# First expert's rows gathered by columns, unread products on TensorE during the top-k, and logits scaled and shifted in one operation per tile

## The chip, the cores and the metric

The kernel runs on one core of one Trainium2 chip. The metric is the device time of one execution in microseconds (us). "PE" is TensorE's matmul stream and "PEld" its weight loads, "DVE" is VectorE, "ACT" is ScalarE, "POOL" is GpSimd, and "SP" is SyncE, whose queue issues the weight transfers. An f32 product of the program appears in the trace as two loads and two matmul instructions (128 instructions for 64 products of one line, say); a transpose appears as one of each.

## The reference, cut to what matters

One encoder block: attention branches, then an expert-choice feed-forward over 16 experts, then a final norm. The change lies between the two halves.

```python
def expert_choice_ffn(h, w_router, w_gate, w_up, w_down):     # h: (1, 512, 1024)
    cap = EC_CAPACITY_FACTOR * S // N_EXPERTS                 # 64 rows for each of 16 experts
    aff = jax.nn.softmax((h @ w_router).astype(jnp.float32), axis=-1)
    gate, idx = lax.top_k(jnp.swapaxes(aff, 1, 2), cap)
    xe = h[bidx, idx]                                         # the rows each expert takes
    hid = (jax.nn.silu(jnp.einsum('becd,edf->becf', xe, w_gate))
           * jnp.einsum('becd,edf->becf', xe, w_up))          # w_gate, w_up: (16, 1024, 2048)
    ye = jnp.einsum('becf,efd->becd', hid, w_down) * gate[..., None]
    return jnp.zeros_like(h).at[bidx, idx].add(ye)
...
h2 = rmsnorm(x, g_norm_ffn[l]) * (1.0 + sc2) + sh2
x = x + gt2 * expert_choice_ffn(h2, ...)
```

## The kernel before

The first 900 us compute the attention half. From about 895 us on the kernel streams the expert weights: 12 tiles of 2 MB for each expert (per quarter of the 1024 inputs one of `w_gate` and one of `w_up`, then four of `w_down`), 192 tiles in all, through a ring of ten slots (`wslot`, `RING`). `loaded` (L1055) asks for the first ten tiles at once; SP's queue issues each later tile in program order, and it waits there until PE has read the tile that its slot held. So the eleventh tile cannot start before the first expert's first gate products (the first 16 instructions of L1199) are done, since they free the first slot.

Between the attention half and those products stands a chain of small steps:

1. `route(j)` gives for each of four tiles of 128 tokens the router's logits `lg[:, j]` and the sum of squares; `rsqrt_mean` makes the reciprocal norm `rs`. L1068 multiplies all logits by `rs`, L1069 adds the row `lbb`. POOL makes the normed tokens `xn` from `rs` at the same time (L1071).
2. Softmax (L1074 to L1079), a transpose on PE (L1084), and the top-k on DVE: eight rounds of `max` (L1089, eight largest) and seven of `match_replace` (L1091). The threshold goes back through PE (L1100) to `thb`; the positions `pos` follow from prefix sums on PE (L1111, L1113) and small DVE steps to L1123.
3. `select(0)` compares `pos` with an iota, four DVE operations (L1141): `gw[:, j]` is a 128 x 64 matrix of zeros and ones, tokens by places.
4. `gather(0, gw)` multiplies it with `xn`: `gw[:, j]` is the stationary operand (64 columns), 512 columns of `xn` move; 8 products, both halves of the array at once. The result `px` holds places by model columns.
5. `rows(px)` copies it to SBUF (L1155), transposes it in four products (L1158), then scales by `a2c` (L1160) and shifts by `sh2c` (L1162) on DVE: `xT[:, k]`, 128 model columns by 64 places, is the stationary operand of every gate and up product.

Two sets of small products that the first expert needs only later, L1207 (`tpb` from `gw` and the identity) and L1213 (`tpb` from `gw` and `aff`), stand between `rows` and the gate products on PE. Where instructions of different steps stand on an engine is decided by the scheduler from the order in which the program is written and from its own forecast of waits.

Of the kernel before, what the change touches and what calls it, by code (L numbers as in the profile page):

```python
# [9 lines left out]
F32 = mybir.dt.float32  # L10
# [4 lines left out]
OP = mybir.AluOpType  # L15
# [4 lines left out]
P = 128  # L20
S = 512
D = 1024
KD = D // P
NT = S // P
# [3 lines left out]
E_N = 16  # L28
CAP = 64
# [72 lines left out]
def tile_block(ctx, tc, x, c, positions, w_ada, b_ada, g_norm_mix, w_in, g_q_lat, g_kv_lat, w_uq, w_ukv,  # L102
               rel_bias, w_out, g_norm_ffn, w_router, w_gate, w_up, w_down, g_final, consts, masks, out):
    nc = tc.nc
    V, A, G, T, SP = nc.vector, nc.scalar, nc.gpsimd, nc.tensor, nc.sync
# [14 lines left out]
    x1 = per.tile([P, NT, D], F32, name="x1")  # L120
# [6 lines left out]
    a2c = per.tile([P, KD], F32, name="a2c")  # L127
# [26 lines left out]
    with ExitStack() as pa:  # L154
# [16 lines left out]
        def sc():  # L171
            return ps.tile([P, 512], F32, name="sc", bufs=3)
# [892 lines left out]

        xn = keep.tile([P, NT, D], F32, name="xn")
        rs = rsqrt_mean(ss2, NT, D, keep, "rs2")
        V.tensor_tensor(lg, lg, rs[:, :, None].to_broadcast([P, NT, E_N]), op=OP.mult)  # L1068
        V.tensor_tensor(lg, lg, lbb[:, None, :].to_broadcast([P, NT, E_N]), op=OP.add)  # L1069
        for j in range(NT):  # L1070
            G.tensor_scalar(xn[:, j], x1[:, j], rs[:, j:j + 1], None, op0=OP.mult)  # L1071
        aff = keep.tile([P, NT, E_N], F32, name="aff")
# [11 lines left out]
            T.transpose(pt[:64, 128 * a:128 * a + 128], afx[:, a], ident)  # L1084
        V.tensor_copy(at, pt[:64, :256])
        m64 = wk.tile([64, CAP], F32, name="m64")
        for r in range(CAP // 8):
            m8 = m64[:, 8 * r:8 * r + 8]
            V.max(m8, at)  # L1089
            if r < CAP // 8 - 1:  # L1090
                V.match_replace(at, m8, at, -1.0)  # L1091
        rev = wk.tile([E_N, CAP], F32, name="rev")
# [7 lines left out]
        T.matmul(pq[:, :E_N], onesr[:E_N], dth, start=True, stop=True)  # L1100
        thb = wk.tile([P, E_N], F32, name="thb")
        V.tensor_copy(thb, pq[:, :E_N])

        ge2 = wk.tile([P, NT, 2, E_N], BF16, name="ge2")
        tb_ = thb[:, None, :].to_broadcast([P, NT, E_N])
# [9 lines left out]
        V.tensor_copy(pre[:, NT, 0], pq[:, 128:144])  # L1115
        eqp = wk.tile([P, NT, E_N], F32, name="eqp")
        V.tensor_tensor(eqp, pre[:, :NT, 1], pre[:, NT, 0][:, None, :].to_broadcast([P, NT, E_N]), op=OP.add)
        t1 = wk.tile([P, NT, E_N], F32, name="t1")
        V.scalar_tensor_tensor(t1, eqp, float(CAP) + 0.5, eqp, op0=OP.is_lt, op1=OP.mult)
        V.tensor_mul(t1, t1, ge2[:, :, 1])  # L1120
# [7 lines left out]
    with ExitStack() as pb_:  # L1128
# [15 lines left out]
        def gather(e, gw):  # L1144
            px = ps.tile([P, 512], F32, name="px", bufs=1)
            for j in range(NT):
                for dh in range(2):
                    T.matmul(px[64 * dh:64 * dh + 64], gw[:, j], xn[:, j, 512 * dh:512 * dh + 512],  # L1148
                             start=j == 0, stop=j == NT - 1)
            return px  # L1150

        def rows(px):

            xe = wbs.tile([P, 4, P], F32, name="xe", tag="xy", bufs=1)
            V.tensor_copy(xe, px.rearrange("q (p r) -> q r p", r=4))  # L1155
            pt = ps.tile([P, 512], F32, name="tpb", bufs=2)
            for n in range(4):
                T.transpose(pt[:, 128 * n:128 * n + 128], xe[:, n], ident)  # L1158
            xT = wbs.tile([P, KD, CAP], F32, name="xT", bufs=1)
            V.tensor_tensor(xT.rearrange("p (h n) s -> p n h s", h=2), pt.rearrange("p (n h s) -> p n h s", n=4, h=2),  # L1160
                            a2c.rearrange("p (h n) -> p n h", h=2)[:, :, :, None].to_broadcast([P, 4, 2, CAP]), op=OP.mult)
            V.tensor_tensor(xT, xT, sh2c[:, :, None].to_broadcast([P, KD, CAP]), op=OP.add)  # L1162
            return xT

        def scatter(se, ye, j, dh):
            pt = ps.tile([P, 512], F32, name="tpb", bufs=2)
            T.matmul(pt, se[:, j], ye[:, dh], start=True, stop=True)  # L1167
            ds_ = slice(512 * dh, 512 * dh + 512)
            V.tensor_add(x1[:, j, ds_], x1[:, j, ds_], pt)  # L1169

        for e in range(E_N):
# [13 lines left out]
            wd = [w_.rearrange("p (r d) -> p r d", r=4) for w_ in wl[8:]]  # L1185
            if e == 0:
                gw = select(0)
                xT = rows(gather(0, gw))

            pg = ps.tile([P, 2, 512], F32, name="pg", bufs=1)  # L1190
            pu = ps.tile([P, 2, 512], F32, name="pu", bufs=1)
# [128 lines left out]
```

## Time and profile before

| what | value |
|---|---|
| median of three runs | 1875.85 us (1874.97 to 1876.68) |
| the profiled execution | 1875.35 us, span in the trace 1873.6 us |
| mean granted clock of TensorE in it | 0.982 |
| PE busy | 1706.3 us, 91% |
| DVE busy | 741.9 us, 40% |
| POOL busy | 155.9 us, 8% |
| bytes moved | 531.33 MB, mean 284 GB/s |

Times in the trace count from the span's start; the time of a run is some 1.75 us longer than the span. The granted clock is 1.00 at 2.4 GHz and 0.50 at 1.2 GHz.

### The profile page before, as it was taken

Reading aid. Unit: us, or ns where it says so; the run is one execution under the profiler, and the core shown is the slowest. Engines: PE = TensorE matmul, PEld = TensorE weight load, DVE = VectorE, ACT = ScalarE, POOL = GpSimd, SP = SyncE. Lnnn points to the kernel's source line nnn. Section 1 sums busy time; section 2 is a strip of 40 time slices with the busy share of each in tenths; the row PEclk is TensorE's granted clock in tenths of the full one; section 3 lists DMA queues with packets and bytes.
Section 4 is the critical chain, followed back from the end, with each engine's and each line's share of the span. In section 5 each row is a group of like instructions: output and inputs, shape, how many; then the busy total and the mean of one; then the engine's idle time right before and its main releaser. Section 6 shows DMA issues by size and latency. Waiting matters only on the chain.

```text
span 1873.6 us, 22273 instructions
## 1 busy us (share of the span) xinstructions
PE 1706.3 (91%) x9196; PEld 1005.1 (54%) x9196; DVE 741.9 (40%) x1393; ACT 392.0 (21%) x768; POOL 155.9 (8%) x148
## 2 busy tenths in 40 slices
PE   3879989999999999999699999999888898889985
PEld 2647668888888888888433333333332333323322
DVE  5877774565554445536612222112221121211213
ACT  3345552232332232223200000000000000000002
POOL 3830000020020001002200000000000000000002
PEclk9989999999999999999899999999999999999998
DMA  9346766535534333232889999999999999999996
GB/s 289 95 140 201 220 188 192 180 107 157 172 113 127 91 90 104 90 84 74 366 363 428 427 427 427 428 427 428 428 426 429 427 427 428 427 427 428 427 424 209
DMA packets 134917, 531.33 MB, mean 284 GB/s; under 512 B 17048, under 2 KB 91288, under 8 KB 108192
## 3 DMA queue, kind: packets, MB, share of 16 engines
q1 hardware_dynamic: 130320, 521.45, 72.0%
q0 software_dynamic: 2080, 6.82, 1.0%
q10 hardware_dynamic: 2416, 1.65, 0.5%
q8 instruction: 72, 1.18, 0.3%
q14 instruction: 29, 0.24, 0.0%
HBM read 520.52 MB, written 16.17 MB: 286 GB/s over the span
## 4 chain that ended last, share of the span: by engine, by line
PE 55%; DMA 30%; DVE 6%; issue 4%; SPq 2%; ACT 1%; POOL 0%; ACTq 0%; DVEq 0%; POOLq 0%
PE pj L455 19%; DMA we<-in_w_up_dram 17%; PE pu L1199 7%; PE pg L1199 6%; PE pj L869 5%; DMA we<-in_w_down_dram 5%; DMA we<-in_w_gate_dram 4%; PE py L1236 4%; PE sc L611 2%; PE px L1148 2%; PE sc L940 2%; DMA x<-bkt_d 2%; PE pj L611 1%; PE tpb L1167 1%; DMA cs<-in_consts_dram 1%
## 5 line engine op out<-in xcount | busy, mean ns | idle before, releaser
L455 PE MATMUL pj<-hh,ws 128*128 128x512 f32 x1152 | 372.0, 398 | 1.7 <-DVE ws L431 1.7
L1199 PE MATMUL pg<-we,xT 128*64 128x512 f32 x1024 | 233.6, 595 | 12.7 <-DMA we<-in_w_gate_dram 12.7
L455 PEld LDWEIGHTS pj<-hh,ws 128*128 128x128 f32 x1152 | 215.8, 188 | 53.6 <-DVE ws L431 2.2
L1199 PE MATMUL pu<-we,xT 128*64 128x512 f32 x1024 | 236.5, 596 | 5.6 <-DMA we<-in_w_up_dram 5.6
L1236 PE MATMUL py<-we,hid 128*64 128x512 f32 x960 | 218.1, 601 | 21.8 <-DMA we<-in_w_down_dram 21.4
L455 PE MATMUL pj<-hl,ws 128*128 128x512 f32 x576 | 229.1, 398 | 0.0
L431 DVE TENSOR_TENSOR ws<-raw,ws 128x1024 fp32r<-128x1024 f32 (+2 forms) x108 | 134.9, 1251 | 130.8 <-ACT ws L430 130.1
L430 ACT ACTIVATE ws<-raw 128x1024 fp32r<-128x1024 f32 (+2 forms) x108 | 111.4, 1033 | 250.9 <-PE pj L455 170.7
L1199 PEld LDWEIGHTS pg<-we,xT 128*64 128x64 f32 x1024 | 72.6, 137 | 153.4 <-issue 131.7
L1236 PEld LDWEIGHTS py<-we,hid 128*64 128x64 f32 x960 | 67.0, 137 | 153.1 <-issue 130.1
L1199 PEld LDWEIGHTS pu<-we,xT 128*64 128x64 f32 x1024 | 71.0, 137 | 144.5 <-issue 129.1
L1169 DVE TENSOR_TENSOR x<-x,tpb 128x512 f32<-128x512 f32 x120 | 77.6, 684 | 130.1 <-PE tpb L1167 130.1
L455 PEld LDWEIGHTS pj<-hl,ws 128*128 128x128 f32 x576 | 108.2, 188 | 24.3
L1221 DVE TENSOR_TENSOR hid<-hid,pu 128x512 f32<-128x512 f32 x32 | 20.6, 683 | 212.5 <-PE pu L1199 212.5
L869 PE MATMUL pj<-ws,hh 128*128 128x256 f32 x512 | 94.4, 282 | 0.0
L869 PEld LDWEIGHTS pj<-ws,hh 128*128 128x128 f32 x512 | 79.4, 188 | 0.0
L1242 DVE SCALAR_TENSOR_TENSOR yf<-py,gv,gt 128x512 f32<-128x512 f32 x15 | 11.3, 751 | 160.0 <-PE py L1236 160.0
L1246 ACT ACTIVATE ye<-yf 64x512 fp32r<-64x512 f32 x30 | 18.9, 628 | 255.7 <-DVE yf L1242 255.3
L1182 POOL COPY we<-gt 64x512 f32<-64x512 f32 x4 | 2.4, 608 | 838.0 <-PE pg L1199 837.9
L869 PE MATMUL pj<-ws,hl 128*128 128x256 f32 x256 | 71.6, 280 | 0.0
L1220 ACT ACTIVATE hid<-pg 128x512 f32<-128x512 f32 x32 | 17.4, 594 | 258.4 <-PE pg L1199 225.2
L1167 PE MATMUL tpb<-ye,se 128*128 128x512 f32 x120 | 51.2, 471 | 13.6 <-DVE x L1169 11.5
(368 smaller groups left out, 1997.7 us busy)
## 6 DMA issues: line engine op xcount, KB each, us to landing
we<-in_w_gate_dram SPq DMA_DIRECT2D x64, 2048.0 KB, 8.0
we<-in_w_up_dram SPq DMA_DIRECT2D x64, 2048.0 KB, 39.1
we<-in_w_down_dram SPq DMA_DIRECT2D x60, 2048.0 KB, 38.0
raw<-in_w_in_dram SPq DMA_DIRECT2D x36, 1024.0 KB, 5.3
raw<-in_w_ada_dram SPq DMA_DIRECT2D x19, 1024.0 KB, 5.4
x<-bkt_d SPq DMA_DIRECT2D x104, 128.0 KB, 4.7
raw<-in_w_in_dram SPq DMA_DIRECT2D x16, 512.0 KB, 5.7
stage_d<-stage POOLq DMA_DIRECT2D x26, 256.0 KB, 5.1
```

Source lines behind the costliest of these rows:

```text
L430: A.activation(dst[:, 0], src, AF.Copy)
L431: V.tensor_sub(dst[:, 1], src, dst[:, 0].bitcast(F32))
L455: T.matmul(pu, parts[k // 4][:, a, k % 4, col:col + 128], hx[b][:, k], start=k == 0 and n == 0, stop=k == KD - 1 and n == 2)
L611: T.matmul(out_, w_(a), b_(b), start=i == 0, stop=i == n_ - 1)
L869: T.matmul(pu[:, 256 * j:256 * j + 256], hx[b][:, k, 128 * m:128 * m + 128], parts[k // 4][:, a, k % 4], start=k == 0 and n == 0, stop=k = ...
L940: T.matmul(o, v_, pT_[:, 128 * k:128 * k + 128], start=first, stop=t_ == 3 and k == 3, skip_group_check=True)
L1148: T.matmul(px[64 * dh:64 * dh + 64], gw[:, j], xn[:, j, 512 * dh:512 * dh + 512], start=j == 0, stop=j == NT - 1)
L1167: T.matmul(pt, se[:, j], ye[:, dh], start=True, stop=True)
L1169: V.tensor_add(x1[:, j, ds_], x1[:, j, ds_], pt)
L1199: T.matmul(acc[64 * hf:64 * hf + 64, b], xT[:, k], w_[:, r, f0:f0 + 512], start=k == 0, stop=k == KD - 1)
L1221: V.tensor_mul(hid[:, b], hid[:, b], pu[:, b].rearrange("q (p r) -> q r p", r=4))
L1236: T.matmul(py[64 * dh:64 * dh + 64], hT[:, g, r], wd[g][:, r, 512 * dh:512 * dh + 512], start=g == 0 and r == 0, stop=g == 3 and r == 3)
```

## The change

It has three parts.

- **Logits.** L1068 and L1069 (two operations on all four tiles) become four operations, one per tile, each of which multiplies by that tile's `rs` and adds `lbb`.
- **Unread products.** `warm` issues products on PE into a PSUM tile (`cold`) that nobody reads: one behind each `max` from the third round on (six), one behind `thb`, two behind the prefix sums. Each has 256 moving columns of `x1` and is two instructions in a trace. Nothing on another engine waits for them.
- **First expert's rows.** `first_rows` replaces `gather` and `rows` for expert 0. Now the columns of `xn` are stationary (128 of them, every fourth one of a half, so that no transpose is needed) and `gw[:, j]` moves (64 columns): 2 halves x 4 columns' residues x 4 token tiles = 32 products. The result lies as `xT` wants it, and eight DVE operations scale and shift it out of PSUM. The other experts keep `gather` and `rows`.

```diff
-        V.tensor_tensor(lg, lg, rs[:, :, None].to_broadcast([P, NT, E_N]), op=OP.mult)
-        V.tensor_tensor(lg, lg, lbb[:, None, :].to_broadcast([P, NT, E_N]), op=OP.add)
+        for j in range(NT):
+            V.scalar_tensor_tensor(lg[:, j], lg[:, j], rs[:, j:j + 1], lbb, op0=OP.mult, op1=OP.add)
...
+        cold = sc()
+        def warm(by, n):
+            for _ in range(n):
+                k = by.shape[0]
+                T.matmul(cold[:by.shape[1], :256], by, x1[:k, 0, :256], start=True, stop=True)
         for r in range(CAP // 8):
             m8 = m64[:, 8 * r:8 * r + 8]
             V.max(m8, at)
+            if r > 1:
+                warm(m8, 1)
             if r < CAP // 8 - 1:
                 V.match_replace(at, m8, at, -1.0)
...
         V.tensor_copy(thb, pq[:, :E_N])
+        warm(thb, 1)
...
+        warm(pre[:, NT, 0], 2)
...
+        def first_rows(gw):
+            xT = wbs.tile([P, KD, CAP], F32, name="xT", bufs=1)
+            for h, nm in enumerate(("px", "py")):
+                pc = ps.tile([P, 512], F32, name=nm, bufs=1)[:, :256].rearrange("p (r s) -> p r s", r=4)
+                for r in range(4):
+                    for j in range(NT):
+                        T.matmul(pc[:, r], xn[:, j, 512 * h + r:512 * h + 512:4], gw[:, j], start=j == 0, stop=j == NT - 1)
+                for r in range(4):
+                    k = 4 * h + r
+                    V.tensor_scalar(xT[:, k], pc[:, r], a2c[:, k:k + 1], sh2c[:, k:k + 1], op0=OP.mult, op1=OP.add)
+            return xT
...
-                xT = rows(gather(0, gw))
+                xT = first_rows(gw)
```

The order of PE's instructions before, from the prefix sums' last product to the first gate products (`px` is the gathered tile, `tpb` the transposes and the two sets of small products, `pg` and `pu` the gate and up products):

```order
L1113 MATMUL tp<-ge_7550,onesb 128x16
L1148 MATMUL px<-xn,gw 64x512 x8
L1158 MATMUL tpb<-cs,xe 128x128 x4
L1207 MATMUL tpb<-cs,gw 64x128 x8
L1213 MATMUL tpb<-aff,gw 64x1 x8
L1199 MATMUL pg<-we_7459,xT 64x512 x8
```

And the same place of the changed kernel (L1093 is `warm`, L1124 was L1113, L1184 is in `first_rows`, L1224 was L1199, L1232 was L1207, L1238 was L1213):

```order
L1124 MATMUL tp<-ge_7560,onesb 128x16
L1093 MATMUL sc<-x_67,pre 16x256 x2
L1184 MATMUL px<-gw,xn 128x64
L1184 MATMUL py<-gw,xn 128x64
L1232 MATMUL tpb<-cs,gw 64x128 x2
L1238 MATMUL tpb<-aff,gw 64x1 x2
L1184 MATMUL px<-gw,xn 128x64
L1184 MATMUL py<-gw,xn 128x64
L1232 MATMUL tpb<-cs,gw 64x128 x2
L1238 MATMUL tpb<-aff,gw 64x1
L1184 MATMUL px<-gw,xn 128x64 x14
L1184 MATMUL py<-gw,xn 128x64 x14
```

The 32 products of `first_rows` stand in one run, with seven of the small products among the first four; the other nine small products have moved behind the first expert's gate and up products. The gate products follow the last product of `py` at once.

On PE ahead of that, from the transposed affinities to the prefix sums, the changed kernel has:

```order
L1084 MATMUL tp<-cs,afx 64x128 x2
L1093 MATMUL sc<-x_67,m_7525 8x256 x6
L1110 MATMUL tp<-dth,onesr 128x16
L1093 MATMUL sc<-x_67,thb 16x256
L1122 LDWEIGHTS ltm
```

Before, L1084 was followed at once by L1100 (now L1110) and that by the loads of `ltm`; the unread products stand between them now, and the prefix sums queue behind the one of `thb`.

## Rows read from the trace of the kernel before

**Rows 1.** Windows by stage: seconds of each engine's work, granted clock, DMA share, GB/s.
```profile
core 0: us, PE busy (x) PEld busy (x) DVE busy (x) ACT busy (x) POOL busy (x), PEclk, DMA share, GB/s
930.00:940.00 10.00, 6.18 (x38) 2.80 (x38) 3.67 (x19) 0.00 (x0) 0.10 (x1) 0.57 1.02 434
940.00:950.00 10.00, 9.14 (x72) 4.13 (x70) 2.88 (x8) 0.58 (x1) 0.00 (x0) 1.00 0.41 123
950.00:1800.00 850.00, 786.10 (x3860) 275.95 (x3858) 168.40 (x306) 61.92 (x105) 2.43 (x4) 1.00 1.01 427
```

**Rows 2.** Timeline of SP's queue: issue time, duration, tile, count.
```profile
918.02 1.22 SPq L1134 DMA_DIRECT2D gt<-mod_d  x2
947.12 3.77 SPq L1052 DMA_DIRECT2D we<-in_w_down_dram  x2
953.99 0.33 SPq L1040 DMA_DIRECT2D we<-in_w_gate_dram  x1
```

**Rows 3.** Timeline from `gw` to the first gate products: start, duration, engine, line, releaser.
```profile
934.70 0.74 DVE L1141 TENSOR_SCALAR gw<-cs,pos 128x64 f32<-128x64 f32 x4
935.10 5.37 PE L1148 MATMUL px<-xn,gw 128*64 128x512 f32 x16 [1.94 <-DVE gw L1141]
941.85 1.10 PE L1207 MATMUL tpb<-cs,gw 128*64 128x128 f32 x16
942.68 0.69 DVE L1162 TENSOR_TENSOR xT<-xT,sh2c 128x512 f32<-128x512 f32 x1
942.77 0.58 PE L1213 MATMUL tpb<-aff,gw 128*64 128x1 f32 x16
943.43 3.65 PE L1199 MATMUL pg<-we,xT 128*64 128x512 f32 x16
```

**Rows 4.** Timeline of stationary loads of 128 f32 columns, at three places.
```profile
592.90 1.54 PEld L1008 LDWEIGHTS tp<-wsh,onesr 128*128 128x128 f32 x12
397.46 0.98 PEld L885 LDWEIGHTS tp<-ex,sel 128*128 128x128 f32 x8
914.33 1.03 PEld L778 LDWEIGHTS tp<-cs,x 128*128 128x128 f32 x8 [0.20 <-issue]
112.11 1.19 PEld L575 LDWEIGHTS tp<-dg,ones 128*128 128x128 f32 x5 [0.52 <-issue]
```

**Rows 5.** Groups by line with shapes kept apart: busy us, mean ns of one.
```profile
L778 PEld LDWEIGHTS tp<-cs,x 128*128 128x128 f32 x32 | 4.7, 206 | 0.9 <-issue 0.6
L885 PEld LDWEIGHTS tp<-ex,sel 128*128 128x128 f32 x32 | 4.4, 193 | 0.3
L575 PEld LDWEIGHTS tp<-dg,ones 128*128 128x128 f32 x8 | 2.0, 328 | 8.0 <-DVE dg L574 6.9 <-issue 1.0
```

**Rows 6.** Timeline of the logits' step, DVE and POOL.
```profile
918.66 0.22 DVE L1068 TENSOR_TENSOR lg<-lg,rs_y 128x64 f32<-128x64 f32 x1
918.74 11.37 POOL L1071 TENSOR_SCALAR xn<-x,rs_y 128x1024 f32<-128x1024 f32 x4 [0.70 <-DVE rs_y L151]
918.92 1.02 DVE L1069 TENSOR_TENSOR lg<-lg,lbb 128x64 f32<-128x64 f32 x1
920.05 0.22 DVE L1074 TENSOR_REDUCE mx<-lg 128x4 f32<-128x64 f32 x1
920.30 0.23 DVE L1075 TENSOR_TENSOR lg<-lg,mx 128x64 f32<-128x64 f32 x1
```

**Rows 7.** Timeline of the top-k's third round and of the steps behind it.
```profile
924.95 0.42 DVE L1089 MAX8 m<-at 64x8 f32<-64x256 f32 x1
925.92 0.42 DVE L1089 MAX8 m<-at 64x8 f32<-64x256 f32 x1
931.23 0.61 PE L1100 MATMUL tp<-dth,onesr 16*128 16x16 f32 x2 [8.70 <-DVE dth L1098]
931.87 0.17 DVE L1102 COPY thb<-tp 128x16 f32<-128x16 f32 x1 [0.70 <-PE tp L1100]
932.49 0.59 PE L1111 MATMUL tp<-ge,ltm 128*128 128x32 bf16 x16 [0.66 <-DVE ge L1107]
933.42 0.16 DVE L1115 COPY pre<-tp 128x16 f32<-128x16 f32 x1
```

**Rows 8.** Windows around falls and rises of the granted clock.
```profile
918.50:919.00 0.50, 0.00 (x0) 0.00 (x0) 0.43 (x4) 0.00 (x0) 0.26 (x1) 1.00 1.07 459
921.50:922.00 0.50, 0.10 (x1) 0.11 (x2) 0.24 (x2) 0.00 (x0) 0.50 (x2) 0.54 0.89 373
938.50:939.00 0.50, 0.50 (x4) 0.19 (x2) 0.00 (x0) 0.00 (x0) 0.00 (x0) 0.89 1.08 459
109.00:112.60 3.60, 2.79 (x7) 1.76 (x8) 1.60 (x11) 0.00 (x0) 0.34 (x2) 0.50 0.20 46
115.50:116.50 1.00, 1.00 (x5) 0.79 (x4) 1.00 (x2) 0.56 (x2) 0.00 (x0) 0.75 0.00 0
```

**Rows 9.** Timeline of a DVE and a POOL operation that overlap, 855 us.
```profile
855.12 4.62 POOL L969 TENSOR_TENSOR raw<-raw,gt 128x2048 f32<-128x2048 f32 x1 [137.96 <-DMA raw<-in_w_out_dram]
856.08 3.68 DVE L845 TENSOR_SCALAR nm<-stt 128x4 f32<-128x4 f32 x1
```

## The prediction

> **What bounds the kernel now.** I read the windows by stage first. From 950 to 1800 us the DMA engines are busy all the time, at 427 GB/s [rows 1]: the stream of expert weights sets the end there, and PE, busy 786 of 850 us, only has to keep up. There is one hole in the stream. Between 940 and 950 us the DMA share is 0.41 [rows 1], so 10 x (1 - 0.41) = 5.9 us of transfer time are lost. SP's queue says why: after the two small `gt` loads at 918.02 it stands still until 947.12, when the first tile beyond the ring's ten is issued [rows 2]. It waits for a slot, and the slot comes free when the first 16 gate instructions end, at 943.43 + 3.65 = 947.08 [rows 3]. Later issues (953.99 and on) come faster than a 2 MB tile needs at 427 GB/s (4.9 us), so the stream does not break again.
>
> So one moment carries the change: the start of the first gate products, 943.43 us [rows 3]. Every microsecond by which it moves up or down moves the rest of the kernel by the same, and no more than 5.9 us can be won, 0.31% of the time. I count everything from there, and call a difference of 0.2% (3.75 us) the least that a measurement of this kernel can tell from no change.
>
> **Logits.** Before, L1068 starts at 918.66 and the next step, L1074, at 920.05: 1.39 us, of which L1069 takes 1.02 us, although it has the shape of L1068, which takes 0.22 [rows 6]. L1069 has two SBUF operands and starts 0.18 us behind POOL's `xn` (918.74); L1075, of the same kind, runs unhindered at 920.30 while POOL still works [rows 6]. So something held L1069 to 919.94 at POOL's start. The four new operations have no row. For their pace I take the four of L1141, 0.74 us [rows 3], 0.185 us each, with 64 columns for their 16. Without a hold they end at 919.4, and L1074 moves up some 0.55 us. With the same hold, which would catch the second one, two more follow it: 0.37 us later than now. They too have two SBUF operands and stand in the same place, so I take +0.2 us, bounds -0.55 and +0.37.
>
> The Trainium skill (SBUF — State Buffer, Who interferes with whom) says that a VectorE operation with two SBUF inputs and a GpSimd operation that reads SBUF exclude each other for a whole instruction. L845 agrees: 3.68 us for four columns, to 859.76, where POOL's operation ends (859.74) [rows 9]. L1069 does not: the rule would have held it to the end of POOL's first `xn` operation, 918.74 + 11.37 / 4 = 921.58, and the trace has 919.94.
>
> **Unread products.** DVE waits for none of them, so the top-k's rounds (0.97 us each, 924.95 to 925.92 [rows 7]) keep their pace. What they change is the clock and what queues behind them on PE. Now the clock is at 1.2 GHz from about 921.5, after an idle stretch that holds 918.5 to 919.0, and goes back to 2.4 GHz only between 938.5 and 939.0, some 3.5 us after `px` started dense work at 935.10 [rows 3, 8]. From the third `max` (ended 925.37) to 931.2 PE would now have a product in every round. A product has two instructions of 256 columns; 16 of 512 columns, two at once, take 3.65 us at 2.4 GHz [rows 3], so one of 256 takes some 0.21 us, a product 0.43, and 0.86 at 1.2 GHz. PE is then nearly filled in each 0.97 us round while the clock is low, for over 5 us. I take it that the clock has risen by 931 us and holds.
>
> Then three effects follow. L1100 and the prefix sums run at the higher clock: an f32 load of 128 columns takes 193 ns at it and 328 ns at the lower one [rows 5], two such loads lie in L1100's 0.61 us [rows 7], and I take -0.2 us for both steps together. The product behind `thb` (ready 932.04) stands in front of the prefix sums, which now start at 932.49 [rows 7]: 932.04 + 0.1 + 0.43 = 932.57, +0.1 us. The two behind `pre` (ready 933.58 [rows 7]) end at 934.5, before `gw` lets PE go on at 935.10 [rows 3]: nothing. Sum -0.1 us. That cover is gone at the lower clock: 933.0 for the prefix sums (+0.5), and 935.9 for the two (+0.3 on top): +0.8 us.
>
> **First expert's rows.** Removed: 943.43 - 935.10 = 8.33 us between the first `px` product and the gate products [rows 3]. Added: 32 f32 products, 64 loads of 128 f32 columns and 64 matmuls of 64 columns. The loads set the pace: 12 of L1008 start within 1.54 - 0.19 us, 0.123 us apart; 8 of L885 0.112 apart, in both cases with only 16 columns moving behind each; 8 of L778, which read `x1` with the same step of four columns that `first_rows` has, 0.117 apart [rows 4, 5]. A matmul of 64 columns (0.05 us) hides under that. I take L778, the only one with the step: 64 x 0.117 = 7.5 us, bounds 7.2 and 7.9. Seven of the 16 small products now stand between them, eight instructions of L1207's 16 (1.10 us) and six of L1213's (0.58) [rows 3]: 0.55 + 0.22 = 0.77 us; before, they lay under DVE's work on `xT` (L1162 ends at 943.37 [rows 3]). The eight DVE operations cost nothing: the gate products begin with `xT[:, 0]`, which is ready while `py` runs, and need `py`'s columns some 7 us later (two groups of gate and up products). Sum 8.3 against 8.33 us: nothing, -0.3 to +0.3.
>
> At 1.2 GHz, L575's loads are (1.19 - 0.33) / 4 = 0.214 us apart [rows 4, 5]: 13.7 us and 1.5 us for the small products, 15.2 in all, +6.9 us.
>
> The Trainium skill (TensorE: Matmul & The Clock Gate, Back-to-back issue gap) gives about 81 ns as the sustained spacing for 128 moving columns, loads included. By it `first_rows` would take 5.2 us in place of 7.5 (an estimate from that page). The three rows above are all slower, with fewer columns moving.
>
> The nine small products that move behind the gate products delay the first expert's own later steps by a microsecond at most. SP's issues are by then ahead of the transfers (a slot freed per 3.43 us, half of a pair of groups that starts at 947.12 and 953.99, against 4.9 us [rows 2]), which hides it.
>
> **Sum.** +0.2 - 0.1 + 0.0 = +0.1 us on the profiled execution's 1875.35 us (span 1873.6 and 1.75 around it), 1875.45. The median of the runs stands 0.5 us higher, which would give 1875.95. I put 1875.6, between them. The change trades DVE steps and transposes for loads of equal length.
>
> **Rivals.**
>
> 1. *The clock rises late.* Windows 109.0 to 112.6 show PE busy 2.79 of 3.6 us, and the rise came only in 115.5 to 116.5, over 6 us after that work began [rows 8]; the unread products might do no better, and the rise may fall into `first_rows`, as it now falls into `px`. Then its start is 0.2 + 0.8 us late, at 936.1; 3.5 us pass at 0.214 (16 instructions), 48 follow at 0.117 (5.6 us), the small products take 1.0: gate products at 946.2, +2.8 us, 1878.4.
> 2. *Slower: the clock stays low through `first_rows`.* Its matmuls cover only 0.05 of each 0.117 us, the rest is loading, and no long stretch of the trace is like it. Start 936.1, 15.2 us: 951.3, +7.9 us; if the gate products also start low, their first group takes 3.65 us more. 1883.5 to 1887. It decides from a pace of 0.117 + 3.7 / 64 = 0.175 us on.
> 3. *The clock is up when `first_rows` starts and falls in it*, for the same reason. With the second half at 0.214: 32 x 0.097 = 3.1 us, and 1.8 to 3.65 us on the first gate group: about 1880.5, just slower.
> 4. *Faster: loads at some 0.08 us.* -2.3 us, and without a hold on the logits -0.75 more: 1872.6. Against it stand the three rows of [rows 4]. To be told from no change it needs another 0.5 us.
> 5. *The logits are held to the end of POOL's first operation*, as L845 was: lg ready at 921.6 for 920.05, +1.5 us, 1877.1. That is the SBUF page's rule. L1069's 1.02 us speak against it.
>
> **Chances.** The forecast 0.49, rival 1 0.18, rival 2 0.13, rival 3 0.07, rival 4 0.08, rival 5 0.05. Rivals 2 and 3 are slower by over 0.2%: 0.20. Most of rival 4, and what I may have overlooked, count as faster: 0.07. The rest, 0.73, is within 0.2%. The range, 1872.5 to 1881, holds the forecast, rivals 1, 3, 4 and 5 and leaves out rival 2. The forecast's own range is 1874.5 to 1876.6.
>
> **What would show it.** Right: granted clock 1.00 from 931 us on without a break; 64 loads 0.11 to 0.12 us apart; gate products within 1 us of 943.4; a DMA hole of 5 to 7 us that ends when their first 16 instructions do. A gate start before 940 or after 947 us makes the forecast wrong, and so does a hole elsewhere in the stream, which would mean that the first gate group is not what the stream waits for.

## The result, and the profile after

The change made the kernel slower: 1889.17 us median (1884.16 to 1892.12, 6 runs) against 1876.26 (1874.97 to 1880.77, 6 runs), a ratio of 1.0066, interval [1.0055, 1.0078]. The forecast was 1875.6 and the top of the range 1881. The profiled execution after took 1892.12 us (span 1890.3), the longest of the six, 16.8 more than the one before.

Windows by stage of the changed kernel, which answer to [rows 1]:

```profile
core 0: us, PE busy (x) PEld busy (x) DVE busy (x) ACT busy (x) POOL busy (x), PEclk, DMA share, GB/s
930.00:940.00 10.00, 8.94 (x39) 2.15 (x40) 7.32 (x30) 0.00 (x0) 4.06 (x2) 0.50 1.00 425
940.00:950.00 10.00, 9.89 (x48) 8.76 (x46) 0.91 (x5) 0.00 (x0) 0.00 (x0) 0.50 0.60 236
950.00:960.00 10.00, 10.00 (x41) 8.65 (x43) 2.20 (x8) 0.00 (x0) 0.00 (x0) 0.50 0.00 0
960.00:970.00 10.00, 10.00 (x48) 3.15 (x46) 0.00 (x0) 0.00 (x0) 0.00 (x0) 0.97 0.60 226
970.00:1800.00 830.00, 768.77 (x3800) 271.33 (x3798) 164.47 (x304) 61.16 (x104) 2.43 (x4) 1.00 1.01 427
```

The hole in the weight stream is 4.0 + 10.0 + 4.0 = 18 us where it was 5.9; behind it the stream moves the same 427 GB/s. PE is busy all the time in the hole, and the clock is at 0.50 through top-k and `first_rows`. SP's queue, which answers to [rows 2]:

```profile
921.93 1.14 SPq L1146 DMA_DIRECT2D gt<-mod_d  x2
963.03 3.77 SPq L1052 DMA_DIRECT2D we<-in_w_down_dram  x2
```

From the `gt` loads to the eleventh tile it now stands still for 41.10 us, before for 29.10. This distance is the measure that I use for all runs below; it starts beside `rs` (POOL's first `xn` operation follows 0.72 us later in both kernels) and ends when the first gate group ends. The timeline of the chain between, which answers to [rows 3, 6, 7]:

```profile
922.58 1.54 DVE L1069 SCALAR_TENSOR_TENSOR lg<-lg,rs_y,lbb 128x16 f32<-128x16 f32 x4
922.65 5.78 POOL L1071 TENSOR_SCALAR xn<-x,rs_y 128x1024 f32<-128x1024 f32 x2 [0.70 <-DVE rs_y L151]
924.22 0.22 DVE L1074 TENSOR_REDUCE mx<-lg 128x4 f32<-128x64 f32 x1
925.82 0.92 DVE L1081 COPY afx<-aff 128x64 f32<-128x64 f32 x1
930.33 5.85 PE L1093 MATMUL sc<-x,m 64*8 64x256 f32 x12 [2.90 <-DVE m L1097]
936.13 0.61 PE L1110 MATMUL tp<-dth,onesr 16*128 16x16 f32 x2
937.00 1.03 PE L1093 MATMUL sc<-x,thb 128*16 128x256 f32 x2 [0.27 <-DVE thb L1112]
937.97 0.61 PE L1122 MATMUL tp<-ge,ltm 128*128 128x32 bf16 x16
939.13 1.89 PE L1093 MATMUL sc<-x,pre 128*16 128x256 f32 x4 [0.47 <-DVE pre L1126]
941.12 0.69 PE L1184 MATMUL px<-gw,xn 128*128 128x64 f32 x2
...
944.81 6.79 PE L1184 MATMUL px<-gw,xn 128*128 128x64 f32 x28
951.40 6.74 PE L1184 MATMUL py<-gw,xn 128*128 128x64 f32 x28
958.06 4.92 PE L1224 MATMUL pg<-we,xT 128*64 128x512 f32 x16
```

Counted from POOL's first `xn` operation (918.74 before [rows 6], 922.65 after), the chain falls behind like this:

| step | before | after | behind |
|---|---|---|---|
| L1074 starts (logits done) | 1.31 | 1.57 | 0.26 |
| product of the threshold on PE starts | 12.49 | 13.48 | 0.99 |
| prefix sums start | 13.75 | 15.32 | 1.57 |
| first `px` product | 16.36 | 18.47 | 2.11 |
| first gate product | 24.69 | 35.41 | 10.72 |
| SP issues the eleventh tile | 28.38 | 40.38 | 12.00 |

`first_rows` takes 958.06 - 941.12 = 16.94 us in place of 8.33, and its loads start (951.40 - 944.81) / 28 = 0.235 us apart (28 instructions, and so 28 loads, of `px` before `py` goes on). The first 16 gate instructions then run at the low clock in part, 4.92 us for 3.65. Of the 16.8 us of the two profiled executions, 12.0 are this; 3.9 lie ahead of the first weight issue, where the change does nothing (those issues start anywhere from 892.9 to 899.0 us in the profiles of this study), and 0.8 behind the eleventh tile.

### The profile page after: what moved, and what is told of

Read it like the earlier page. It is cut to its first block, busy times and chain, and to the rows that moved or that the text cites. A ratio compares the mean times of both kernels' runs of the same rounds, so it can differ in the third digit from the quotient of the medians.

```text
span 1890.3 us, 22402 instructions
## 1 busy us (share of the span) xinstructions
PE 1726.5 (91%) x9258; PEld 1021.1 (54%) x9258; DVE 744.1 (39%) x1400; ACT 392.3 (21%) x768; POOL 156.6 (8%) x148
## 4 chain that ended last, share of the span: by engine, by line
PE 54%; DMA 34%; DVE 5%; issue 4%; SPq 1%; ACT 1%; POOL 0%; ACTq 0%; DVEq 0%; POOLq 0%
PE pj L455 19%; DMA we<-in_w_up_dram 14%; DMA we<-in_w_gate_dram 8%; DMA we<-in_w_down_dram 6%; PE pu L1224 5%; PE pg L1224 5%; PE pj L869 5%; PE py L1261 4%; PE sc L611 2%; PE sc L940 2%; PE pj L611 1%; DMA x<-bkt_d 1%; PE px L1160 1%; DMA cs<-in_consts_dram 1%; PE sc L833 1%
## 5 line engine op out<-in xcount | busy, mean ns | idle before, releaser
L1224 PE MATMUL pg<-we,xT 128*64 128x512 f32 x1024 | 235.8, 598 | 13.8 <-DMA we<-in_w_gate_dram 13.8
L1224 PE MATMUL pu<-we,xT 128*64 128x512 f32 x1024 | 236.4, 596 | 7.4 <-DMA we<-in_w_up_dram 7.4
L1224 PEld LDWEIGHTS pg<-we,xT 128*64 128x64 f32 x1024 | 73.2, 137 | 156.2 <-issue 131.2
L1224 PEld LDWEIGHTS pu<-we,xT 128*64 128x64 f32 x1024 | 70.9, 137 | 146.1 <-issue 130.0
L1207 POOL COPY we<-gt 64x512 f32<-64x512 f32 x4 | 2.4, 608 | 850.9 <-PE pg L1224 850.8
```

Source lines behind the costliest of these rows:

```text
L1224: T.matmul(acc[64 * hf:64 * hf + 64, b], xT[:, k], w_[:, r, f0:f0 + 512], start=k == 0, stop=k == KD - 1)
```

## The experiments

Each row is one kernel; "distance" is SP's from the `gt` issue to its next one, in that kernel's profile, then its difference to the 29.10 of before; the times are medians in us, beside before's on the same chip. The probe of the loads, told further down, holds PE up and is not in it.

| kernel | distance | to before | time, before's | ratio, interval |
|---|---|---|---|---|
| change | 41.10 | +12.00 | 1889.17, 1876.26 | 1.0066 [1.0055, 1.0078] |
| logits alone | 31.27 | +2.17 | 1877.96, 1875.94 | 1.0012 [1.0001, 1.0024] |
| unread products alone | 29.44 | +0.34 | 1876.92, 1875.94 | 1.0001 [0.9989, 1.0014] |
| `first_rows` alone | 39.67 | +10.57 | 1885.69, 1875.94 | 1.0049 [1.0031, 1.0067] |
| wide unread products | 42.53 | +13.43 | 1888.67, 1875.94 | 1.0070 [1.0048, 1.0092] |
| clock held, `first_rows` | 40.07 | +10.97 | 1888.21, 1875.73 | 1.0067 [1.0045, 1.0089] |
| clock held, gather | 30.21 | +1.11 | 1877.84, 1875.73 | 1.0009 [0.9997, 1.0022] |
| logits, `xn` on ACT | 31.87 | +2.77 | 1879.52, 1875.73 | 1.0015 [1.0000, 1.0029] |
| logits, `xn` on ACT, clock held, gather | 31.91 | +2.81 | 1878.51, 1875.73 | 1.0016 [1.0002, 1.0030] |
| columns side by side | 42.78 | +13.68 | 1888.71, 1875.86 | 1.0056 [1.0034, 1.0079] |
| columns side by side, clock held | 32.58 | +3.48 | 1881.90, 1875.86 | 1.0030 [1.0018, 1.0042] |
| logits, `xn` on ACT behind the Exp, fewer unread columns, gather | 26.48 | -2.62 | 1875.33, 1875.86 | 0.9998 [0.9989, 1.0008] |

Time and distance go together within some 2.6 us, so the distance is where most of the time is lost. The distance is that of one execution, though, and a part of it moves by about a microsecond: `gather`'s 16 instructions of `px` start at the low clock, the clock rises while they run, and they take 5.37 us before, 6.55 with the logits alone and 5.89 with `xn` on ACT, two edits that leave PE's work alone. A difference of one microsecond between such kernels says little by itself.

**Each part alone.** The first three of these kernels each take one part of the change. The logits:

> The kernel before with the logits' step alone changed. From the profile after: the four operations took 1.54 us where the two took 1.26, and the copy behind the softmax 0.92 us where it took 0.20, which together put the top-k 1.0 us later. If these four operations are the cause, this kernel is 0.3 to 1.0 us slower than before. The rival (the hold of about 0.8 us falls wherever POOL starts, whatever DVE runs) gives 0.2 to 0.4 us. Either is too small for the clock of the runs; the profile's distance from the norm's last step to the first max (before 918.48 to 923.02) decides.

```profile
918.15 1.54 DVE L1069 SCALAR_TENSOR_TENSOR lg<-lg,rs_y,lbb 128x16 f32<-128x16 f32 x4
918.23 8.59 POOL L1071 TENSOR_SCALAR xn<-x,rs_y 128x1024 f32<-128x1024 f32 x3 [0.69 <-DVE rs_y L151]
921.39 0.92 DVE L1081 COPY afx<-aff 128x64 f32<-128x64 f32 x1
```

The timeline of that kernel (DVE and POOL) repeats what the changed kernel shows: the four operations take 1.54 us, and a second hold has appeared, 0.92 us on the `afx` copy, which now comes 0.3 us after POOL's second operation has begun (918.23 + 8.59 / 3 = 921.09). Together they put the threshold's product 0.97 us later (13.46 us behind POOL's first operation for 12.49). The other 1.2 of the +2.17 us is `px`, which takes 6.55 us: here the clock is still at 0.50 at 941 us. That this comes of the logits' edit is not shown; what the holds cost is about 1.0 us, the upper end of the expectation.

The unread products:

> The kernel before with the nine unread products alone. If they leave TensorE's clock at half, as in the changed kernel, the prefix sums and the gathering start 0.5 to 1.1 us later and nothing comes back: +0.5 to +1.5 us. If they do raise it here (the gathering then takes 3.5 us for 5.4), -1 to -2 us.

They do not raise the clock: it stays at 0.50 until 938.8 us (before: 938.6), when `px` is running. `px` starts 1.1 us later behind POOL's first operation than before, takes 4.61 us for 5.37, and little is won or lost (+0.34).

`first_rows`:

> The kernel before with first_rows alone, no unread product. Theory: the clock is at half all through first_rows, with or without the unread products, and the 64 loads lie 0.234 us apart as in the changed kernel: 64 x 0.234 = 15 us and 1.5 to 1.8 for the small products, so +8 to +9 us, and up to 1.5 more for a gate group at half clock: +8 to +10.5 us. Rival: the unread products are what costs, and first_rows alone is within 2 us of before.

It carries most of the 12.00 us: +10.57 (the three parts alone add up to 13.08, so they are not strictly additive). It takes 16.94 us here too (935.33 to 952.27), at clock 0.50 throughout.

**Are the products too narrow?** Their stationary operand has 8 or 16 columns. Here it has 128:

```diff
...
+            T.matmul(cold[:by.shape[1], :8], by, x1[:k, 0, :8], start=True, stop=True)
             for _ in range(n):
...
-                T.matmul(cold[:by.shape[1], :256], by, x1[:k, 0, :256], start=True, stop=True)
+                T.matmul(cold[:, :256], x1[:, 0, 256:384], x1[:, 0, :256], start=True, stop=True)
```

> The changed kernel with the same nine unread products at the same places, but with 128 partitions and 128 stationary columns where there were 64 or 128 partitions and 8 or 16 columns (a tiny product of 8 columns ahead of each keeps the wait). If the narrow products are why the clock stayed at half, it rises during the top-k, first_rows runs with loads 0.117 us apart, and the time is within 2 us of before. If the width does not matter, the clock stays at half and the time is 10 to 13 us above before, as in the changed kernel. If loads with a step of four columns are slow at any clock, the clock rises and the loads still lie over 0.2 us apart.

Windows on PE of that kernel:

```profile
core 0: us, PE busy (x), PEclk, DMA share, GB/s
924.00:932.00 8.00, 7.74 (x25) 0.50 1.00 426
937.00:953.00 16.00, 15.90 (x68) 0.50 0.17 62
```

PE is busy nearly without a gap from 924 to 932, and in `first_rows` behind it, and the clock stays at 0.50. The narrow stationary operand of these products was not what kept it low; what did is not shown.

**Hold the clock.** Unread products of 512 columns with 128 stationary columns of `x1`, each set behind a tiny product of the value that it waits for, from `rs` on, before the clock falls (five there, one in each round, one of 256 columns behind `thb`, one of 512 behind `pre`):

```diff
...
+        warm(rs, 5)
...
-            if r > 1:
-                warm(m8, 1)
+            warm(m8, 1)
```

> The changed kernel with more for PE to do: five f32 products of 512 columns right behind rs, one of 512 in each of the eight rounds of the top-k, one of 256 behind thb, one of 512 behind pre, all with 128 stationary columns of x1 and each set behind a tiny product of the value it follows. Their results are not read. The number to look at is the distance from the start of POOL's first xn operation to the first gate product: 24.7 us before, 35.5 us with the change. Theory (the clock is the cause): it stays at 1.00 from rs on, first_rows takes 7.5 to 8.5 us, the gate products start 25 to 26.5 us behind, their first group takes 3.65 us, and the time is within 1.5 us of before's. Rival (loads with little moving do not hold the clock): it is 1.00 until first_rows and falls inside it; the gate start is 29 to 33 us behind and the time 4 to 8 us over before's. Second rival (the loads with a step of four columns are slow by themselves): the clock is 1.00 and the loads still start 0.23 us apart, the gate start is some 33 us behind, the time some 8 us over before's.

Windows of PE's weight loads and the timeline of `first_rows`:

```profile
core 0: us, PEld busy (x), PEclk, DMA share, GB/s
918.00:937.00 19.00, 7.01 (x76) 1.00 1.01 427
937.00:941.00 4.00, 3.48 (x15) 1.00 0.96 396
941.00:942.00 1.00, 1.00 (x6) 0.89 0.59 127
942.00:953.00 11.00, 10.83 (x50) 0.50 0.01 4
```

```profile
937.55 7.70 PE L1185 MATMUL px<-gw,xn 128*128 128x64 f32 x32 [0.21 <-DVE gw L1154]
945.05 7.67 PE L1185 MATMUL py<-gw,xn 128*128 128x64 f32 x32
952.65 1.12 PE L1225 MATMUL pg<-we,xT 128*64 128x512 f32 x2
```

My theory fell here. The clock is 1.00 until about 941.8, and the 15 loads up to 941 fill 3.48 us of PEld, 0.23 us each; the first half, in which the clock falls, runs at (945.05 - 937.55) / 32 = 0.234 us a load, and the second half, at 0.50, at (952.65 - 945.05) / 32 = 0.237. The pace of these loads hardly depends on the clock. The second rival of that expectation held in its mechanism (the gate products start 34.3 us behind POOL's first operation, about 33 expected), though the time is 12.5 us over before's for some 8. The clock also falls in `first_rows`, as the first one said, but that costs mainly the first gate group, 5.01 us for 3.65. Of the +10.97 us, `first_rows` is 6.77 (15.10 us for 8.33), the first gate group 1.37, and 2.83 come from a later start, of which the next kernel shows the cause.

The same products with gather in place of `first_rows`:

> As the run before with the same unread products, but with before's gather and rows for the first expert in place of first_rows; the new logits stay. Theory: the clock is up when px starts, so its 16 instructions take 3.5 us where they took 5.4, and the gate products start 23.5 to 24.5 us behind POOL's first xn operation (24.7 before: +1.0 for the logits and the afx copy, -1.9 for px, -0.2 for the loads behind the top-k). Time 0 to 1.5 us under before's, which the times alone do not tell from no change. Rival (the unread products stand in the way on PE and give back what px wins): 24.7 to 26 us, time up to 1.5 us over before's.

The clock is 1.00 throughout, `px` takes 3.65 us, and yet the distance is 1.11 longer. A set of a tiny product and one of 512 columns takes PE 1.18 us, a round of the top-k 0.97, so PE arrives at the threshold's product 1.8 us later than in the change (15.29 us behind POOL's first operation, 13.48 there). An unread product costs nothing only while PE has time for it.

**What slows the loads.** The probe measures them by themselves:

```diff
...
+        for st in (1, 4, 2, 0, 1, 4):
...
+                if st == 1:
+                    T.matmul(pb[:, :64], x1[:, 2, 0:128], x1[:, 0, :64], start=True, stop=True)
+                elif st == 2:
+                    T.matmul(pb[:, :64], x1[:, 2, 0:256:2], x1[:, 0, :64], start=True, stop=True)
+                elif st == 4:
+                    T.matmul(pb[:, :64], x1[:, 2, 0:512:4], x1[:, 0, :64], start=True, stop=True)
+                else:
+                    T.transpose(pb[:, :128], x1[:, 2, 0:512:4], ident)
```

> The loads by themselves, at the high clock: the kernel before with six groups of unread f32 products right behind rs. In each group three of 512 columns come first, then eight with 64 moving columns and 128 stationary columns of x1, in a step of 1, 4, 2, then eight transposes with a step of 4, then 1 and 4 again. PE is held up by some 30 us; its time is not to be compared. Theory (the step slows a load of a product, of which there are two, but not that of a transpose): about 0.12 us between loads for step 1, 0.23 for step 4, 0.12 to 0.23 for step 2, 0.12 for the transposes, which are what the prediction took its pace from. Rival (the step does nothing): 0.23 us for all three steps, or 0.12 for all three.

Its timeline on PE, at clock 1.00 (L1075 has step 1, L1079 step 4, L1077 step 2, L1081 are the transposes, L1072 what stands between):

```profile
925.50 1.89 PE L1075 MATMUL sc<-x 128*128 128x64 f32 x16
927.23 2.79 PE L1072 MATMUL sc<-x 128*128 128x512 f32 x6
929.86 3.72 PE L1079 MATMUL sc<-x 128*128 128x64 f32 x16
933.41 2.79 PE L1072 MATMUL sc<-x 128*128 128x512 f32 x6
936.04 1.99 PE L1077 MATMUL sc<-x 128*128 128x64 f32 x16
937.87 2.79 PE L1072 MATMUL sc<-x 128*128 128x512 f32 x6
940.50 1.12 PE L1081 MATMUL sc<-cs,x 128*128 128x128 f32 x8
941.45 2.74 PE L1072 MATMUL sc<-x 128*128 128x512 f32 x6
```

From the first of a group to what follows: step 1, 1.73 / 16 = 0.108 us a load; step 2, 1.83 / 16 = 0.114; step 4, 3.55 / 16 = 0.222; transposes with step 4, 0.95 / 8 = 0.119. The groups that come again show the same (1.89 and 3.72 us). So the step of four doubles the time from one load of a product to the next. The transposes with that step read the same 128 f32 columns of the same tile and stay at 0.119. Transposes without a step are not in the probe, but the kernel before has them, at clock 1.00:

```profile
974.48 0.86 PEld L1228 LDWEIGHTS tpb<-cs,hid 128*128 128x128 f32 x8 [0.81 <-issue]
```

With 0.14 us for one load they start (0.86 - 0.14) / 7 = 0.103 us apart, so the step adds 0.016 us to a transpose and 0.114 to a product's load. Why the two differ is not shown: they are other kinds of instruction, and the transposes also move 128 columns where the products move 64.

The Trainium skill (TensorE: Matmul & The Clock Gate, LDWEIGHTS) gives the time of a load by its number of columns alone. The rows of step 1 and 4 have the same number and differ by a factor of two; the measurement decides.

**Take the step away.** `xn` is stored so that the columns of one residue lie side by side, the rest of the change as it is:

```diff
...
-            G.tensor_scalar(xn[:, j], x1[:, j], rs[:, j:j + 1], None, op0=OP.mult)
+            G.tensor_scalar(xn[:, j].rearrange("p (h r q) -> p h r q", h=2, r=4),
+                            x1[:, j].rearrange("p (h q r) -> p h r q", h=2, r=4), rs[:, j:j + 1], None, op0=OP.mult)
...
-                        T.matmul(pc[:, r], xn[:, j, 512 * h + r:512 * h + 512:4], gw[:, j], start=j == 0, stop=j == NT - 1)
+                        T.matmul(pc[:, r], xn[:, j, 512 * h + 128 * r:512 * h + 128 * r + 128], gw[:, j], start=j == 0, stop=j == NT - 1)
```

> The changed kernel with xn stored so that the 128 columns of each stationary operand of first_rows lie side by side, and not in a step of four (POOL's operations read x1 in that order, rows copies px accordingly; the result is the same). The unread products are the change's own, so the clock is low when first_rows starts. Theory (the step is what slows the loads, at either clock): they start closer together than 0.234 us, 0.12 to 0.21, first_rows is 3 to 8 us shorter, and the time is 3 to 9 us under the change's 1889, about 1880 to 1886. Rival (the low clock or the shape of 64 moving columns sets the pace): still 0.23 us or more, time as the change's. In both, POOL's operations might become longer; up to 3 us more each is hidden before px needs xn.

```profile
944.98 6.23 PE L1185 MATMUL px<-gw,xn 128*128 128x64 f32 x28
951.00 6.18 PE L1185 MATMUL py<-gw,xn 128*128 128x64 f32 x28
```

Neither theory is quite right: at the low clock the loads now start (951.00 - 944.98) / 28 = 0.215 us apart, just below 0.235. `first_rows` is 1.3 us shorter (15.66 us), and POOL's operations, which read in the step now, take back more than that: they last 3.81 us each for 2.9, DVE is held longer beside them (2.40 us on the logits, 1.96 on the copy), and `px` starts 2.6 us later than in the change. With the clock held as well:

> The same storage of xn with the unread products of 512 columns that kept the clock at 1.00 until 941 us in an earlier run. Theory (the step): at the high clock the loads start 0.11 to 0.13 us apart, first_rows takes 7 to 8.5 us in place of 15.1, the clock may still fall inside it, and the time is within 3 us of before's. Rival (64 moving columns behind a load of 128 are this slow by themselves): 0.23 us apart again and 1887 to 1889.

```profile
939.15 3.76 PE L1186 MATMUL px<-gw,xn 128*128 128x64 f32 x32 [0.21 <-DVE gw L1155]
942.75 3.74 PE L1186 MATMUL py<-gw,xn 128*128 128x64 f32 x32
946.41 1.08 PE L1226 MATMUL pg<-we,xT 128*64 128x512 f32 x4
```

Now, at clock 1.00, they are (942.75 - 939.15) / 32 = 0.113 us apart, and `first_rows` takes 7.26 us. The time is 6.0 us over before's, twice the 3 that I had expected as the most. In the profile the longer holds and the late PE of the held clock come first (the threshold's product starts 16.98 us behind POOL's first operation; 12.49 before), which makes the distance 3.48 longer. That profile is of a run of 1878.93 us, and the ten runs lie between 1877.99 and 1886.00; what the longer ones lose beyond the 3.48 is not seen in it.

**The holds on DVE.** The logits with `xn` made by ACT:

> The kernel before with the logits part of the change alone, and xn made by ACT (four operations behind its Exp) in place of POOL. The number to look at is the distance from the end of rs to the first max: 6.3 us before, 7.3 us with the logits part alone. Theory (POOL's operations hold the DVE operations that read two SBUF operands, and the afx copy): the four operations take 0.6 to 0.75 us together, the afx copy 0.2, and the distance is 5.4 to 5.8 us. Rival (four operations take 0.37 us each by themselves): they still take 1.5 us, and the distance is 6.3 to 7.3. Against both: xn might come too late for px if an ACT operation takes over 2.5 us. Time 0 to 1 us under before's by the theory, 0 to 1 over by the rival; only the trace tells these apart.

```profile
919.27 0.67 DVE L1069 SCALAR_TENSOR_TENSOR lg<-lg,rs_y,lbb 128x16 f32<-128x16 f32 x4
...
923.71 0.22 DVE L1077 TENSOR_REDUCE mx<-lg 128x4 f32<-128x64 f32 x1 [3.19 <-ACT lg L1074]
924.51 0.20 DVE L1081 COPY afx<-aff 128x64 f32<-128x64 f32 x1
```

Without POOL beside them the four operations take 0.67 us and the copy 0.20: the theory on the holds is right. The time is not lower because the scheduler put ACT's four `xn` operations (4.26 us) in front of the Exp, and DVE waits 3.19 us. The next kernel has the same fault, and PE is late behind its unread products as well: the threshold's product starts 17.1 us behind the end of `rs`, 14.9 in this one. So the rival of its expectation held: the gate products start 27.6 us behind `rs`, where the theory had 22 to 23:

> All together but first_rows: the new logits, xn on ACT, the unread products that are to hold the clock, before's gather and rows. Theory: gate products 22 to 23 us behind the end of rs (24.8 before: -0.7 for the logits without POOL beside them, -1.9 for px at the high clock, -0.2 for the loads); time 2 to 3 us under before's, about 1873. Rival (the clock falls in spite of the unread products, or PE is late with them): 24 us or more, and no difference in time.

The last one orders `xn` behind the Exp by a scale that depends on the reciprocal, and gives PE fewer unread columns:

```diff
...
+        V.scalar_tensor_tensor(rsl, mx1, 0.0, rs, op0=OP.mult, op1=OP.add)
+        for j in range(NT):
+            A.mul(xn[:, j], x1[:, j], rsl[:, j:j + 1])
...
+            if r < CAP // 8 - 1:
+                warm(m8, 1, 448)
```

> A try at a faster version: before's gather and rows; the new logits with xn made by ACT behind its Exp (ordered by a scale that is formed from rs after the reciprocal), so that nothing stands in front of the Exp; unread products that hold the clock but let PE go in time (three of 512 columns behind rs, one of 448 in each of seven rounds, none behind the threshold, one of 512 behind pre). Theory: four logits operations in 0.67 us and the afx copy in 0.20, px in 3.65 us for 5.37, so the gate products start 22 to 23 us behind the end of rs (24.8 before); 2 to 2.8 us under before's time, about 1873.3. Rival (PE gets late behind the unread products, or the ring's hole does not shrink): 24 us or more, time as before's.

```profile
932.58 3.65 PE L1163 MATMUL px<-xn,gw 128*64 128x512 f32 x16 [0.21 <-DVE gw L1156]
939.18 1.08 PE L1227 MATMUL pg<-we,xT 128*64 128x512 f32 x4
```

Every step of its timeline is as the theory says: the gate products start 22.2 us behind `rs` (24.8 before [rows 3, 6]), and the distance is 2.62 us shorter. Yet the median is only 0.5 us lower, and the interval takes in no change and leaves out the 2.6 us. From the eleventh tile's issue to the end this profile has 928.6 us; that of before has 926.5, those of the other kernels in the table 926.6 to 927.5. SP's queue shows where this goes, though not why: the issues are 4.24 us ahead of before's at the eleventh tile (942.88 and 947.12), 4.04 at 1201.69, and 1.97 at the last weights (1795.58 and 1797.55), so the lead shrinks inside the weight stream, while the DMA engines are busy all the time in both kernels. The cause stays open, and no version is shown to beat the kernel before.

## Why the prediction was wrong

- **What bounds the kernel** was right: in all kernels the time follows the start of the first gate products, and the hole in the stream is the loss.
- **First expert's rows: the step that failed is "I take L778, the only one with the step: 64 x 0.117 = 7.5 us".** L778 has the step but is a transpose (and moves 128 columns, where the prediction says that all three rows move fewer). In a product the same operand's loads start 0.222 to 0.237 us apart, at either clock, so the 64 loads take 14.2 to 15.2 us. This alone makes the change slower: with the clock high when it starts, `first_rows` still takes 15.10 us for 8.33, 6.77 of that kernel's +10.97. Bounds of 7.2 and 7.9 came from rows with no product that has the step; the operation had no row, and the bounds should have said so. The small products in between took 1.46 us at the low clock (942.22 to 942.95 and 944.08 to 944.81) where the sum had 0.77.
- **Unread products: the step "I take it that the clock has risen by 931 us and holds" failed too.** It stayed at 0.50 to 960; why is not shown. By itself that would have cost nearly as much: without the step the loads are 0.215 us apart at the low clock. Either fault hides the other. `first_rows` takes 16.94 us in the change, 15.10 with the clock up when it starts, 15.66 without the step, and 7.26 with both undone, near the 7.5 that the sum gave its loads. (The small products stand among its products in the first and third of these, not in the others.) The distances of those kernels, +10.97, +13.68 and +3.48, also hold what the cures cost.
- **Rival 2** gave the right place and nearly the price (+7.9 to +11.5 us, 1883.5 to 1887; measured +12.0 and 1889.17, both just above it), with a chance of 0.13. Its ground, the clock, is half of the cause: its 0.214 us was taken from loads without the step. Rivals 1 and 3 did not happen; by its own terms, 3.1 and up to 3.65 us, rival 3 reaches 1882.4, beyond the range that was said to hold it. Rival 4 (loads near 0.08) is refuted by the probe's 0.108, and rival 5 by L1074, which starts 1.57 us behind POOL where it would have been 2.8.
- **Logits: mis-sized.** The term was +0.2 us, bounds -0.55 and +0.37. The four operations cost +0.26, but the same shift pushes the `afx` copy under POOL's second operation: 0.92 us for 0.20, in all +0.99. The part counted the wait at one place and did not ask what the shift brings behind POOL's next operation. L845, which it took as a row that agrees with the exclusion of operations with two SBUF inputs, is a TENSOR_SCALAR with one, so that row says nothing of two.
- **The queue behind `thb` and `pre`** was priced nearly rightly for the low clock: +0.8 us said, (1.57 - 0.99) + (2.11 - 1.57) = 1.1 measured.

The Trainium skill (SBUF — State Buffer, Who interferes with whom) names copies, too, as operations that can contend with GpSimd under some conditions on their operands; the `afx` copy agrees (0.92 us beside POOL's operation, 0.20 without). That the loser waits for the whole instruction does not hold here: the hold on the four operations is 1.54 - 0.67 = 0.87 us beside an operation of 2.9.

## What to carry to other kernels

Before an operand's pace is taken from another row, its access pattern and its kind of instruction must both be the same: a transpose's load is no evidence for a product's. Where a step of the forecast needs two things to go right (here the clock and the pace), each failure alone may cost nearly the whole, and experiments that undo one at a time may show almost nothing; undo both. And with a held clock the old gather is still shorter than `first_rows` at its best (939.18 - 932.58 = 6.60 us against 7.26), so loads of 128 columns for 64 moving ones are a poor trade on this chain.

## What the runs showed of the hardware

- Loads of 128 f32 columns in products with 64 moving columns start 0.108 us apart with step 1, 0.114 with step 2 and 0.222 with step 4 at the high clock (probe), and 0.215 and 0.235 with steps 1 and 4 at the low one. Transposes start 0.119 us apart with step 4 (probe) and 0.103 without (before, L1228).
- The granted clock beside unread products: in the kernel of wide products, with 256 columns each, PE was busy 7.74 of the 8 us from 924 to 932, and the clock was 0.50. In the run that held the clock, with products of 512 columns, it was 1.00 from 918 to 941. With columns side by side and the same products of 512 it had fallen to 0.50 by 919 and was back at 1.00 from 922 on:

```profile
core 0: us, PE busy (x), PEclk, DMA share, GB/s
919.00:921.00 2.00, 2.00 (x4) 0.50 0.99 421
922.00:939.00 17.00, 15.24 (x70) 1.00 1.00 425
939.00:946.50 7.50, 7.35 (x66) 1.00 0.34 118
```

- In the same kernel the clock stayed at 1.00 through the 7.26 us of `first_rows`; with the step of four, in the run that held the clock, it fell inside `first_rows`.
- POOL's operations on 1024 columns take 2.9 us, and 3.8 when they read with a step of four; the holds on DVE grow with them (1.54 to 2.40 us for the four logits operations, 0.92 to 1.96 for the `afx` copy). The Trainium skill (GPSIMD Engine Reference, Performance pitfalls for Q7 kernels) names such a step as costly, by about half; here it is a third.
